# Windowed attention in a decoder layer: the weighted sums of values computed per half of a query block, with a difference over 64 keys in quarters of the TensorE array

## The chip, the core and the metric

The kernel runs on one core of one Trainium2 chip. Five engines work side by side, each with its own instruction queue: TensorE (PE in the profile; PEld are its weight loads), VectorE (DVE), ScalarE (ACT), GpSimd (POOL) and SyncE (SP, which here only issues DMAs). The metric is the time of one execution in microseconds on the device; less is better.

## What is computed

One decoder layer over 2048 tokens of width 1024. A joint input projection feeds a sliding-window attention (8 query heads, 2 key/value heads, width 64, blocks of 128 queries) and a convolution group; both are joined by an output projection, and a gated feed-forward network follows, each with root-mean-square norms around it. The part that matters here is the attention, in the reference:

```
kb, vb = band(kp), band(vp)            # previous block and own block: 256 keys
s = einsum("bnqhgd,bnkhd->bnhgqk", qb, kb) * scale
dist = qi + BLOCK - kj                 # qi: 0..127, kj: 0..255
in_band = (dist >= 0) & (dist < WINDOW)   # WINDOW = BLOCK = 128
s = where(valid, s + bias, -inf)
...
p = (p / denom)
o = einsum("bnhgqk,bnkhd->bnqhgd", p, vb)
```

With a window of 128 and blocks of 128, query q of a block sees exactly 128 keys: keys 0 to q of its own block, and keys q+1 to 127 of the previous block. So for each key place k from 0 to 127 there is one weight: it belongs to the own block's key k where k <= q, and to the previous block's key k where k > q.

## The kernel before

The layer runs in stages over four groups of 512 tokens. Stage A is the projections (PSUM banks `mm`, four of them), stage B the attention, C the convolution's taps on VectorE and its tail, J a product of two weight matrices, W the output projection and first norms, H and F the start of the feed-forward network, G its end. Stages A, W, J and F are long runs of matmuls of 128x128 weights by 512 columns. Stage B and the others are written as generators and woven into these runs in lanes; at the end a scheduler with a timeline of its own (`schedule_with_timeline_sim=True`, L1635) decides each engine's order from priorities and from when tiles come free. Each engine then runs its queue strictly in that order.

Stage B (`stage_b`, L465) has four blocks of 128 queries for each of the four groups, sixteen in all. For each block:

- `front(b)`, L472: two groups of score matmuls (output `tr@B`, inputs `kz` and `ql@A`, 64 rows of the array for each key/value head `g`, twelve matmuls a group, in one PSUM bank for each `g`), then VectorE keeps for each key place the score of the block it belongs to (L501), adds the bias and takes maxima (L504), and ScalarE takes exponentials (L524).
- `back(b)`, L531: VectorE forms `vd`, the previous block's values less the own block's (128x128, L538 through the helper at L85); it divides the weights by their sum; for each of the two heads `g`, TensorE turns four 128x128 pieces (L546), ScalarE copies the bank to `pg[:, 1]` (L547), which holds all weights with keys on partitions and 4 x 128 queries as columns, and GpSimd makes `pg[:, 0]` from it, the same with zeros where k <= q (L549).
- Then the weighted sum (L567 through `mat`, L108): in one bank, own values times all weights plus `vd` times the masked weights. `g` takes one half of the array's columns, since the values of a head are 64 wide. This is four matmuls of 128 rows, 64 columns of weights and 512 columns of data; they are plain float32, and each stands in the trace as two records. ScalarE copies the bank to `at` (L576) and issues its DMA to `mixT` (L578).
- The very first block of all has no previous block; it has only the two matmuls with the own values.

The banks called `tr` (L75) are three; the transposes of a block, its weighted sum and the score groups take them in turn. A score group needs two.

Of the kernel before, what the change touches and what calls it, by code (L numbers as in the profile page):

```python
# [17 lines left out]
AF = mybir.ActivationFunctionType  # L18
ALU = mybir.AluOpType
# [6 lines left out]
P = 128  # L26
# [2 lines left out]
KC = D // P  # L29
NF = DFF // P  # L30
TAPS = 31
HALO = TAPS - 1
EPS = 1e-6
NEG = -1e30
# [3 lines left out]
def layer_kernel(ctx, tc, x, xT, cols, rows, sinks, relb, onehot, w_in, w_four, w_pw, w_out, w_gate, w_up, w_down, out):  # L38
    nc = tc.nc
# [35 lines left out]
    tr = lambda: bank("tr", 3)  # L75
# [3 lines left out]
    act = nc.scalar.activation  # L79
# [27 lines left out]
    def mat(*args, **kw):  # L107
        r = nc.tensor.matmul(*args, **kw)  # L108
        if not inlane[0]:
            lead_pe[0] = r  # L110
        return r
# [353 lines left out]
    def stage_b(t):  # L465
        L = f"B{t}"
        q = qs[t]

        def freed(r):
            done_.append(r)  # L470

        def front(b):  # L472
            lab[0] = L
            first = t == 0 and b == 0
            tok = slice(b * P, (b + 1) * P)
            win = slice(b * P, b * P + 256)
            mx = sm(8)
            pr = f4("p", (P, 8, P))
            for ip in range(2):
                os = [tr().rearrange("p (j k) -> p j k", j=2) for _ in range(2)]  # L480
                lead = []
                pq = tc.cur_priority
                for j in range(2):
                    i = 2 * ip + j
                    for n, (a, k) in enumerate(((0, 0), (0, 1), (1, 0))):
                        for g in (1, 0):
                            sl = slice(64 * g, 64 * g + 64)
                            if lead:
                                tc.cur_priority = pq - 10000
                            r = mat(os[g][:, j], q[i][sl, a, tok], kz[sl, k, win], start=n == 0, stop=n == 2)  # L490
                            if lead:
                                after_first(lead[-1], r)
                            else:
                                for x_ in done_[-3:][:2]:
                                    after_first(x_, r, mybir.DependencyClass.Sync)
                            if len(lead) < 2:
                                lead.append(r)
                tc.cur_priority = pq + 1
                for g in range(2):
                    prev = neg.unsqueeze(2).to_broadcast([P, 2, P]) if first else os[g][:, :, 0:P]  # L500
                    nc.vector.copy_predicated(os[g][:, :, P:], upper.unsqueeze(1).to_broadcast([P, 2, P]), prev)  # L501
                    for j in range(2):
                        h = 4 * g + 2 * ip + j
                        read = nc.vector.tensor_tensor_reduce(  # L504
                            out=pr[:, h],
                            in0=os[g][:, j, P:],
                            in1=bias[0][:, h],
                            op0=ALU.add,
                            op1=ALU.max,
                            scale=1.0,  # L510
                            scalar=NEG,
                            accum_out=mx[:, h : h + 1],
                        )
# [12 lines left out]
            rd = sm(8)  # L526
            nc.vector.reciprocal(rd, den)
            live[b] = pr, rd
            yield YC

        def back(b):  # L531
            pr, rd = live.pop(b)
            first = t == 0 and b == 0
            pt = []
            if not first:
                lab[0] = L
                vd = t_("vd", (P, P))
                vtt(vd, vtok[:, b], vtok[:, b + 1], ALU.subtract)  # L538
            for g in range(2):
                lab[0] = L  # L540
                hs = slice(4 * g, 4 * g + 4)
                vtt(pr[:, hs], pr[:, hs], rd[:, hs].unsqueeze(2).to_broadcast([P, 4, P]), ALU.mult)
                pg = f4("p", (P, 2, T))
                o = tr()
                for i in range(4):
                    nc.tensor.transpose(o[:, i * P : (i + 1) * P], pr[:, 4 * g + i], ident)  # L546
                freed(act(pg[:, 1], o, AF.Copy))  # L547
                if not first:
                    nc.gpsimd.affine_select(  # L549
                        out=pg[:, 0].rearrange("p (i q) -> p i q", q=P),  # L550
                        in_=pg[:, 1].rearrange("p (i q) -> p i q", q=P),
                        compare_op=ALU.is_gt,
                        fill=0.0,
                        base=0,
                        pattern=[[0, 4], [-1, P]],
                        channel_multiplier=1,
                    )
                pt.append(pg)
                yield 0.9
            yield YP  # L560
            lab[0] = L
            o = tr()
            lead = None
            for kb in (1,) if first else (0, 1):
                for g in (1, 0):
                    sl = slice(64 * g, 64 * g + 64)
                    r = mat(o[sl], vtok[:, b + 1, sl] if kb else vd[:, sl], pt[g][:, kb], start=first or kb == 0, stop=kb == 1)  # L567
                    if lead is None:
                        lead = r
                        pq = tc.cur_priority  # L570
                        tc.cur_priority = pq - 10000
                    else:
                        after_first(lead, r)
            tc.cur_priority = pq
            at = f2("at")
            freed(act(at, o, AF.Copy))  # L576
            c0 = t * T + b * P
            nc.scalar.dma_start(  # L578
                mixT[0:4, :, c0 : c0 + P].rearrange("c p t -> p c t"), at.rearrange("p (c t) -> p c t", c=4)
            )  # L580
            yield 1.8

        live = {}

        def scores():
            for b in range(4):
                yield from front(b)
                if 0 < b < 3:
# [1051 lines left out]
```

## Time and profile before

| | |
|---|---|
| time, median of 3 runs | 1907.33 us (1906.63 to 1907.36) |
| profiled execution: span from first to last instruction | 1907.9 us; its own time is not listed beside it |
| granted TensorE clock | 0.999 |
| instructions in the span | 26569 |
| ACT busy | 970.6 us (51%) |
| POOL busy | 179.2 us (9%) |
| weighted sums, records on PE | 64 with `vtok`, 60 with `vd` |
| first and last weighted sum start | 128.2 us and 552.9 us |
| score groups, records on PE | 384, from 77.2 us to 521.3 us |

Busy shares of an engine say how much of the span it had work in hand. TensorE's matmuls are pipelined, so their recorded lengths overlap: a record of a 512-column matmul lasts about 390 ns while the next one starts about 227 ns after it. What a matmul costs is therefore read from where the next one starts, not from its length.

### The profile page before, as it was taken

What the parts mean: (1) busy time and instruction counts of PE and PEld (TensorE: products, weight loads), DVE (VectorE), ACT (ScalarE), POOL (GpSimd) and SP (SyncE); (2) the same over time, 40 slices, a digit from 0 to 9 for tenths busy, and PEclk for the clock granted to TensorE, in tenths of its full rate; (3) what the DMA queues carried; (4) which work ended last, traced back from release to release, by engine and by line L of the source; (5) the groups of instructions that cost most, each with busy time, mean ns of one, the idle gap of its engine ahead of it and who ended that gap; (6) DMA issues with size and microseconds to landing.
All of it is one profiled execution on the core that took longest, in us unless ns stands there. A gap on an engine that the chain in (4) does not pass through costs nothing.

```text
span 1907.9 us, 26569 instructions
## 1 busy us (share of the span) xinstructions
PE 1889.1 (99%) x8714; PEld 1530.1 (80%) x8714; DVE 1490.7 (78%) x2721; ACT 970.6 (51%) x1912; POOL 179.2 (9%) x196
## 2 busy tenths in 40 slices
PE   9999999999999999999999999999999999999998
PEld 8777777777777888888888878788888888888886
DVE  6999999987966999999996765887567674455558
ACT  5356445566667433433445574685443433345452
POOL 2010001110000000000000000010033233211002
PEclk9999999999999999999999999999999999999999
DMA  9887746679688677877776596798554443375663
GB/s 353 300 281 238 248 160 207 230 228 318 218 274 276 232 234 232 293 261 243 244 268 195 196 326 212 259 333 307 166 176 156 160 138 127 116 258 187 206 220 133
DMA packets 226491, 439.29 MB, mean 230 GB/s; under 512 B 22536, under 2 KB 48560, under 8 KB 226352
## 3 DMA queue, kind: packets, MB, share of 16 engines
q1 hardware_dynamic: 207344, 411.37, 64.8%
q10 hardware_dynamic: 17088, 19.93, 2.9%
q0 software_dynamic: 1920, 6.29, 0.9%
q8 instruction: 68, 1.11, 0.2%
q14 instruction: 71, 0.58, 0.1%
HBM read 318.48 MB, written 119.02 MB: 229 GB/s over the span
## 4 chain that ended last, share of the span: by engine, by line
PE 78%; DVE 9%; DMA 8%; ACT 3%; issue 2%; SPq 0%; ACTq 0%; DVEq 0%; POOL 0%; POOLq 0%
PE mm@F L108 34%; PE mm@G L108 16%; PE mm@A L108 14%; PE tr@W L108 5%; PE mm@W L108 3%; PE tr@B L108 2%; PE ct@J L108 1%; DVE w@F L85 1%; DVE mid@W L85 1%; DMA hl@A<-x 1%; DVE sm@G L85 1%; DVE y2@C L85 1%; DMA chl@H<-hT 1%; DVE hl@G L85 1%; DMA chl@F<-w_gate 1%
## 5 line engine op out<-in xcount | busy, mean ns | idle before, releaser
L108 PE MATMUL mm@F<-hl@H,w@F 128*128 128x512 f32 x1056 | 255.8, 391 | 1.8 <-ACT mm@F L1058 1.6
L108 PEld LDWEIGHTS mm@F<-hl@H,w@F 128*128 128x128 f32 x1056 | 197.7, 188 | 44.8 <-ACT mm@F L1058 2.8
L108 PE MATMUL mm@G<-hl@G,hl@G 128*128 128x512 f32 x924 | 226.1, 393 | 2.3 <-ACT hl@G L904 1.5
L904 ACT ACTIVATE w@F<-chl@F 128x512 fp32r<-128x512 f32 x220 | 136.5, 626 | 170.2 <-PE mm@F L108 158.7
L108 PEld LDWEIGHTS mm@G<-hl@G,hl@G 128*128 128x128 f32 x924 | 171.5, 188 | 39.7 <-ACT hl@G L904 2.2
L108 PE MATMUL mm@G<-w@G,hl@G 128*128 128x512 f32 x876 | 199.8, 389 | 0.6 <-DVE w@G L85 0.6
L108 PEld LDWEIGHTS mm@G<-w@G,hl@G 128*128 128x128 f32 x876 | 164.3, 188 | 35.2 <-DVE w@G L85 1.0
L108 PE MATMUL mm@A<-hl@A,w@A 128*128 128x512 f32 x792 | 192.2, 394 | 0.0
L108 PEld LDWEIGHTS mm@A<-hl@A,w@A 128*128 128x128 f32 x792 | 146.8, 188 | 32.5 <-issue 1.7
L85 DVE TENSOR_TENSOR w@F<-chl@F,w@F 128x512 fp32r<-128x512 f32 x198 | 148.1, 753 | 25.5 <-ACT w@F L904 25.0
L85 DVE SCALAR_TENSOR_TENSOR y2@C<-g2@C,colt,y2@C 128x1024 f32<-128x1024 f32 x120 | 154.0, 1283 | 0.2
L108 PE MATMUL mm@F<-mid@H,w@F 128*128 128x512 f32 x528 | 130.6, 390 | 1.0 <-DVE w@F L85 0.9
L108 PE MATMUL mm@F<-ql@H,w@F 128*128 128x512 f32 x528 | 129.7, 390 | 0.2
L108 PE MATMUL mm@F<-p@H,w@F 128*128 128x512 f32 x528 | 129.1, 389 | 0.0
L108 PE MATMUL mm@F<-x@H,w@F 128*128 128x512 f32 x528 | 127.8, 390 | 0.0
L108 PEld LDWEIGHTS mm@F<-mid@H,w@F 128*128 128x128 f32 x528 | 98.8, 188 | 22.2 <-DVE w@F L85 1.3
L108 PEld LDWEIGHTS mm@F<-ql@H,w@F 128*128 128x128 f32 x528 | 98.7, 188 | 21.3 <-DVE w@F L85 0.6
L108 PEld LDWEIGHTS mm@F<-x@H,w@F 128*128 128x128 f32 x528 | 98.7, 188 | 21.3 <-issue 0.8
L108 PEld LDWEIGHTS mm@F<-p@H,w@F 128*128 128x128 f32 x528 | 99.1, 188 | 20.6
L133 ACT ACTIVATE w@A<-raw@A 128x512 fp32r<-128x512 f32 x100 | 60.9, 625 | 80.2 <-PE mm@A L108 46.3
L85 DVE TENSOR_TENSOR w@G<-raw@G,w@G 128x512 fp32r<-128x512 f32 x72 | 50.2, 698 | 64.2 <-ACT w@G L904 63.4
L108 PE MATMUL mm@W<-w@W,hl@W 128*128 128x512 f32 x384 | 97.1, 399 | 0.8 <-DVE x@W L85 0.4
(322 smaller groups left out, 3363.9 us busy)
## 6 DMA issues: line engine op xcount, KB each, us to landing
mids<-fa@F SPq DMA_DIRECT2D x154, 256.0 KB, 3.3
raw@A<-w_in SPq DMA_DIRECT2D x50, 512.0 KB, 4.9
w@A<-lo_in SPq DMA_DIRECT2D x84, 256.0 KB, 4.0
fa@G<-mids SPq DMA_DIRECT2D x74, 256.0 KB, 4.7
fc@G<-mids SPq DMA_DIRECT2D x72, 256.0 KB, 3.5
w@W<-lo_out SPq DMA_DIRECT2D x48, 256.0 KB, 4.8
chl@F<-w_gate SPq DMA_DIRECT2D x22, 512.0 KB, 4.4
raw@F<-w_gate SPq DMA_DIRECT2D x22, 512.0 KB, 4.2
```

Of the source, the lines that this page charges most:

```text
L85: r = op(*args, **kw)
L108: r = nc.tensor.matmul(*args, **kw)
L133: act(w[:, 0], raw, AF.Copy)
L904: act(w[:, 0], x, AF.Copy)
```

## The change

For the first 64 queries of a block (half n = 0), keys 64 to 127 always belong to the previous block; for the last 64 queries (n = 1), keys 0 to 63 always belong to the own block. So the base of half 0 is now the previous block's values and the base of half 1 the own block's, and the difference is needed only over 64 keys: keys 0 to 63 for half 0, keys 64 to 127 for half 1, with opposite signs. The sums of the two halves go to two banks of 256 columns each. A difference matmul then has 64 rows, 64 columns of weights and 256 columns of data, a quarter of the array; a base matmul has 128 rows, 64 columns and 256 columns of data. `vd` is made by two VectorE instructions on 64 partitions each, the masked weights by two GpSimd instructions of half the columns each, and ScalarE copies two banks of 256 columns instead of one of 512.

```diff
@@ stage_b
+        def quarter(pg, kb, n):
+            return pg[:, kb].rearrange("p (i q) -> p i q", q=P)[:, :, H * n : H * n + H]
...
                 vd = t_("vd", (P, P))
-                vtt(vd, vtok[:, b], vtok[:, b + 1], ALU.subtract)
+                vtt(vd[0:H], vtok[0:H, b + 1], vtok[0:H, b], ALU.subtract)
+                vtt(vd[H:P], vtok[H:P, b], vtok[H:P, b + 1], ALU.subtract)
...
                 if not first:
-                    nc.gpsimd.affine_select(
-                        out=pg[:, 0].rearrange("p (i q) -> p i q", q=P),
-                        in_=pg[:, 1].rearrange("p (i q) -> p i q", q=P),
-                        compare_op=ALU.is_gt,
...
+                    for n, cmp in enumerate((ALU.is_ge, ALU.is_gt)):
+                        nc.gpsimd.affine_select(
+                            out=quarter(pg, 0, n),
+                            in_=quarter(pg, 1, n),
+                            compare_op=cmp,
+                            fill=0.0,
+                            base=-H * n if n else 0,
+                            pattern=[[0, 4], [-1 if n else 1, H]],
+                            channel_multiplier=1 if n else -1,
+                        )
...
-            o = tr()
+            os = [tr()[:, 0 : 4 * H] for _ in range(2)]
             lead = None
             for kb in (1,) if first else (0, 1):
-                for g in (1, 0):
-                    sl = slice(64 * g, 64 * g + 64)
-                    r = mat(o[sl], vtok[:, b + 1, sl] if kb else vd[:, sl], pt[g][:, kb], start=first or kb == 0, stop=kb == 1)
...
+                for n in range(2):
+                    for g in (1, 0):
+                        sl = slice(H * g, H * g + H)
+                        rows_ = slice(0, P) if kb else slice(H * n, H * n + H)
+                        v = vtok[:, b + (n or first), sl] if kb else vd[rows_, sl]
+                        r = mat(os[n][sl], v, quarter(pt[g], kb, n)[rows_], start=first or kb == 0, stop=kb == 1)
...
             at = f2("at")
-            freed(act(at, o, AF.Copy))
+            for n in range(2):
+                freed(act(at.rearrange("p (i q) -> p i q", q=P)[:, :, H * n : H * n + H],
+                          os[n].rearrange("p (i q) -> p i q", q=H), AF.Copy))
```

`H` is 64. The scheduler places the eight matmuls of a block in three ways. The lists below are TensorE's queue; in them `tr@B_224` and so on are banks, `p@B` the weights of one head, `mm@A`, `mm@F` outputs of stages A and F, and a row's size is that of its output. The helper `mat` stands at L108 before and at L109 after the change.

First, the last block of the first 512 tokens. Before, its sum and the start of the next score group:

```order
L108 MATMUL mm@A_344_2184<-hl@A_284_1812,w@A_343_2181 128x512 x2
L108 MATMUL tr@B_281_1795<-p@B_272_1737,vd@B_269_1725 64x512
L108 MATMUL tr@B_281_1795<-p@B_270_1728,vd@B_269_1725 64x512
L108 MATMUL tr@B_281_1795<-p@B_272_1737,vtok 64x512
L108 MATMUL tr@B_281_1795<-p@B_270_1728,vtok 64x512
L108 MATMUL tr@B_313_1996<-kz,ql@A_268_1722 128x256
```

The same place with the change:

```order
L109 MATMUL mm@A_348_2215<-hl@A_295_1892,w@A_347_2212 128x512 x3
L109 MATMUL tr@B_284_1820<-p@B_275_1761,vd@B_272_1747 64x256
L109 MATMUL tr@B_284_1820<-p@B_273_1751,vd@B_272_1747 64x256
L109 MATMUL tr@B_285_1821<-p@B_275_1761,vd@B_272_1747 64x256
L109 MATMUL tr@B_285_1821<-p@B_273_1751,vd@B_272_1747 64x256
L109 MATMUL tr@B_284_1820<-p@B_275_1761,vtok 64x256
L109 MATMUL tr@B_284_1820<-p@B_273_1751,vtok 64x256
L109 MATMUL tr@B_285_1821<-p@B_275_1761,vtok 64x256
L109 MATMUL tr@B_285_1821<-p@B_273_1751,vtok 64x256
L109 MATMUL mm@A_363_2295<-hl@A_265_1703,w@A_361_2289 128x512 x3
```

All four difference matmuls stand together, then the four base matmuls; nine of the fifteen blocks that have a difference are like this. The score group that came straight behind the sum now comes later, with 19 projection matmuls ahead of it. Over the whole queue, eight sums were followed straight by a score group before, and one is now.

Second, the second block of all, with the change (before, its four matmuls stood together, with a score group straight behind):

```order
L109 MATMUL tr@B_225_1448<-p@B_223_1439,vd@B_215_1383 64x256
L109 MATMUL tr@B_225_1448<-p@B_216_1387,vd@B_215_1383 64x256
L109 MATMUL tr@B_225_1448<-p@B_223_1439,vtok 64x256
L109 MATMUL tr@B_225_1448<-p@B_216_1387,vtok 64x256
L109 MATMUL mm@A_282_1792<-mid@A_104_714,w@A_280_1786 128x512
...
L109 MATMUL mm@A_282_1792<-chl@A_127_871,w@A_281_1789 128x512
L109 MATMUL tr@B_226_1449<-p@B_223_1439,vd@B_215_1383 64x256
L109 MATMUL tr@B_226_1449<-p@B_216_1387,vd@B_215_1383 64x256
L109 MATMUL tr@B_226_1449<-p@B_223_1439,vtok 64x256
L109 MATMUL tr@B_226_1449<-p@B_216_1387,vtok 64x256
L109 MATMUL tr@B_237_1510<-kz,ql@A_99_694 128x256
```

The two halves stand apart, with 17 projection matmuls between them. Three blocks are split like this (the others with 3 and with 8 matmuls between the halves).

Third, the last block of all. Before:

```order
L108 MATMUL tr@B_977_5660<-p@B_972_5632,vd@B_969_5620 64x512
L108 MATMUL tr@B_977_5660<-p@B_970_5623,vd@B_969_5620 64x512
L108 MATMUL tr@B_977_5660<-p@B_972_5632,vtok 64x512
L108 MATMUL tr@B_977_5660<-p@B_970_5623,vtok 64x512
L108 MATMUL mm@F_1017_5908<-x@H_863_5137,w@F_1007_5844 128x512 x3
```

With the change:

```order
L109 MATMUL tr@B_992_5793<-p@B_987_5764,vd@B_984_5750 64x256
L109 MATMUL tr@B_992_5793<-p@B_985_5754,vd@B_984_5750 64x256
L109 MATMUL tr@B_992_5793<-p@B_987_5764,vtok 64x256
L109 MATMUL tr@B_992_5793<-p@B_985_5754,vtok 64x256
L109 MATMUL tr@B_993_5794<-p@B_987_5764,vd@B_984_5750 64x256
L109 MATMUL tr@B_993_5794<-p@B_985_5754,vd@B_984_5750 64x256
L109 MATMUL tr@B_993_5794<-p@B_987_5764,vtok 64x256
L109 MATMUL tr@B_993_5794<-p@B_985_5754,vtok 64x256
```

The halves follow each other without other work between them, but each half's base stands ahead of the other half's difference. The last three blocks are like this (in the first of them one base matmul of half 0 stands ahead of the difference of half 1, the other behind it).

More of the change, by code (lines that the diff above doesn't have):

```diff
@@ L31 @@
 TAPS = 31
+H = P // 2
 HALO = TAPS - 1
@@ L548, in back @@
                 if not first:
-                    nc.gpsimd.affine_select(
-                        out=pg[:, 0].rearrange("p (i q) -> p i q", q=P),
-                        in_=pg[:, 1].rearrange("p (i q) -> p i q", q=P),
-                        compare_op=ALU.is_gt,
[L553 to L557, printed above, removed]
+                    for n, cmp in enumerate((ALU.is_ge, ALU.is_gt)):
[8 more added lines that the diff above has]
+                        )
                 pt.append(pg)
@@ L561, in back @@
             lab[0] = L
-            o = tr()
+            os = [tr()[:, 0 : 4 * H] for _ in range(2)]
             lead = None
             for kb in (1,) if first else (0, 1):
-                for g in (1, 0):
-                    sl = slice(64 * g, 64 * g + 64)
-                    r = mat(o[sl], vtok[:, b + 1, sl] if kb else vd[:, sl], pt[g][:, kb], start=first or kb == 0, stop=kb == 1)
[L568 to L573, printed above, removed]
+                for n in range(2):
[4 more added lines that the diff above has]
+                        r = mat(os[n][sl], v, quarter(pt[g], kb, n)[rows_], start=first or kb == 0, stop=kb == 1)
+                        if lead is None:
+                            lead = r
+                            pq = tc.cur_priority
+                            tc.cur_priority = pq - 10000
+                        else:
+                            after_first(lead, r)
             tc.cur_priority = pq
             at = f2("at")
-            freed(act(at, o, AF.Copy))
+            for n in range(2):
+                freed(act(at.rearrange("p (i q) -> p i q", q=P)[:, :, H * n : H * n + H],
+                          os[n].rearrange("p (i q) -> p i q", q=H), AF.Copy))
             c0 = t * T + b * P
```

## The prediction

> **What bounds the kernel now.** I read the busy times first, then what TensorE (PE) waited for, then the timeline of one weighted sum. The page's first part:
>
> ```profile
> PE 1889.1 (99%) x8714; PEld 1530.1 (80%) x8714; DVE 1490.7 (78%) x2721; ACT 970.6 (51%) x1912; POOL 179.2 (9%) x196
> ```
>
> PE's recorded lengths overlap, so 99% alone proves little. The view of waits, for PE over the whole span, has fourteen rows; the first and the last two are
>
> ```profile
> PE ct@X L108 <- POOL ident masks.py:199: 1.6, 1, 1.6
> ...
> PE mm@F L108 <- ACT gb@F L1159: 0.2, 1, 0.2
> PE tr@B L546 <- DVE sm@B L504: 0.2, 1, 0.2
> ```
>
> They fall from 1.6 to 0.2 us and together make about 10 us of 1907.9. PE has work nearly everywhere, so what counts is how long its own queue takes: a microsecond that the change adds to that queue or takes from it is a microsecond of the result. The sums are few:
>
> ```profile
> L108 PE MATMUL tr@B<-p@B,vtok 128*64 128x512 f32 x64 | 16.5, 594 | 0.0
> L108 PE MATMUL tr@B<-p@B,vd@B 128*64 128x512 f32 x60 | 16.2, 618 | 0.0
> ```
>
> 33 us of PE in all, of which the difference (`vd`) is half. Halving that half could not gain more than 8 us, 0.4%.
>
> What one sum costs is read from starts. This is PE's timeline, and that of its weight loads, at the second block:
>
> ```profile
> 152.00 1.29 PE L108 MATMUL mm@A<-chl@A,w@A 128*128 128x512 f32 x5
> 153.22 1.08 PE L108 MATMUL tr@B<-p@B,vd@B 128*64 128x512 f32 x4
> 154.13 1.03 PE L108 MATMUL tr@B<-p@B,vtok 128*64 128x512 f32 x4
> 155.09 0.97 PE L108 MATMUL tr@B<-kz,ql@A 64*128 64x256 f32 x12
> 155.99 1.19 PE L108 MATMUL mm@A<-chl@A,w@A 128*128 128x512 f32 x4
> ```
> ```profile
> 153.22 0.20 PEld L108 LDWEIGHTS tr@B<-p@B,vd@B 128*64 128x64 f32 x4 [0.35 <-issue]
> 153.70 0.14 PEld L108 LDWEIGHTS tr@B<-p@B,vtok 128*64 128x64 f32 x2 [0.29 <-issue]
> 154.13 0.14 PEld L108 LDWEIGHTS tr@B<-p@B,vtok 128*64 128x64 f32 x2 [0.28 <-issue]
> ```
>
> Two matmuls (one for each head, in the two column halves) are four records, and they run in **rounds** of two at a time: the loads for the base come at 153.70 and 154.13, one round or 0.43 us apart. From the first `vd` record to the first `vtok` record is 0.91 = two rounds and 0.05; from there to the score group 0.96 = two rounds and 0.10. Ahead of the sum, five projection records of about 0.39 us start within 1.29 - 0.39 = 0.90, so every 0.225; the last starts at 152.90, and the sum 0.32 behind it, 0.095 more than the rule. So **entering** this shape costs 0.095 + 0.05 = 0.145 us and **leaving** it 0.10. Behind the score group four projection records take 1.19 - 0.39 = 0.80 for three steps instead of 0.675: the first weights of a new shape, 128 columns wide, cost another 0.125, against 0.05 for 64 columns. A change back to 128x128 is then about 0.22, one to the score shape (weights of 128 columns too) about 0.2. Between rounds of one shape nothing of this is paid.
>
> The Trainium skill has this as a rule: in "TensorEngine Tiling (Array Packing)", section "Tiling Modes", a change of tiling mode, not merely of the tile, drains the TensorE. The 0.095 and 0.10 at these borders agree. It names no price; with a drain alone, without the weights' 0.05, the inner changes below would be 24 x 0.095 = 2.3 us and the sum +1.4.
>
> **The change, term by term.**
>
> 1. *Streaming.* A round of 256 columns should be half of 0.43, 0.215 us. In nine blocks the four quarter matmuls stand together, and I take them to run all four at once: two rounds of 0.215 instead of two of 0.43, -0.43 each, **-3.9**. In the six others (three split, three with the halves in a row) only two difference matmuls are neighbours: four rounds of 0.215, 0.86 as before. In one of these a base matmul of half 0 is cut off from its partner: ten rounds of 0.215 = 2.15 against 4 x 0.43 = 1.72, **+0.4**. The base of all sixteen blocks goes from two rounds of 0.43 to four of 0.215: nothing. No row shows a plain float32 round of 256 columns. A projection step, one pass of 512 columns, takes 0.225, and half a plain float32 round of 512 columns 0.215; if each short round had that 0.01 as a fixed part, 108 rounds would add 1.1; less than half of 0.43 is excluded, since the columns still have to pass. I take 0, since the rounds of 0.43 are the nearest row. That four quarters run at once is not in the trace either: two column halves do (above), and two row halves do, as twelve score records in 0.97 us show, 0.28 us being the last one's own length:
>
> ```profile
> L108 PE MATMUL tr@B<-kz,ql@A x384: 271/277/385, 77.2 to 521.3; 64*128 64x256 f32 x192
> ```
>
>    Its ends are two rounds (-3.9) and four (0).
>
> 2. *Changes of shape inside a sum.* The difference (64 rows) and the base (128 rows) are now different shapes. The order has 24 such borders: one in each of nine blocks, two in each split block, three in each of the last three. From below 0, if a change of rows alone is free; from above 0.22, the dearest border seen. I take 0.145, as for entering this shape with the same 64 columns of weights: **+3.5** (0 to 5.3).
>
> 3. *Split blocks.* A second entry and a second return to 128x128 in three blocks: 3 x (0.145 + 0.22) = **+1.1**.
>
> 4. *Score groups that move away.* Eight groups started straight behind a sum, sharing its border. Seven now stand behind projection matmuls: the sum returns to 128x128 (0.22 for 0.2), and the group has a border of its own, 7 x 0.2, with the rounding **+1.5**.
>
> Together -3.9 + 0.4 + 3.5 + 1.1 + 1.5 = **+2.6 us** on PE.
>
> The other engines:
>
> ```profile
> L85 DVE TENSOR_TENSOR vd@B<-vtok x15: 273/283/292, 95.0 to 514.4; 128x128 f32<-128x128 f32 x15
> L576 ACT ACTIVATE at@B<-tr@B 128x512 f32<-128x512 f32 x16 | 9.4, 590 | 12.0 <-PE tr@B L108 12.0
> L549 POOL TENSOR_SCALAR_AFFINE_SELECT p@B<-p@B x30: 633/838/1802, 142.6 to 552.2; 128x512 f32<-128x512 f32 x30
> 148.05 0.87 POOL L549 TENSOR_SCALAR_AFFINE_SELECT p@B<-p@B 128x512 f32<-128x512 f32 x1 [4.47 <-ACT p@B L547]
> ```
>
> DVE makes `vd` in two instructions of the same 128 columns on 64 partitions: between 0 and 0.28 more for each block, 4.2 us in all. It is formed early (the first at 95.0, for the sum at 153.2), and DVE's queue is filled up by convolution taps that nothing waits for at once, so I count 0. That cover is thin in two stretches:
>
> ```profile
> 144.00:192.00 48.00, 48.00 (x233) 36.72 (x232) 47.89 (x107) 29.81 (x77) 3.31 (x3) 1.00 0.74 243
> 288.00:336.00 48.00, 48.00 (x252) 36.99 (x251) 47.75 (x105) 26.76 (x61) 6.62 (x10) 1.00 0.68 214
> ```
>
> The third figure of time is DVE's, full to 0.3 us; four sums lie there, so 4 x 0.28 = 1.1 if the cover fails. ScalarE's copy becomes two of 256 columns, each between half and all of 0.59: 0 to +9 us on an engine that is half idle; 0. GpSimd's select becomes two of 256 columns, again between half and all of 0.84; in this block it ended at 148.9, 4.3 us ahead of the sum, so even doubled it is hidden.
>
> **Rivals.**
>
> *The four quarters go two at a time.* Term 1 loses its -3.9: +6.5, **1913.8**, slower. For it: no row shows four at once, and each matmul brings two records that must follow each other. Against it: in the old sum those records pair up across column halves. It decides at the nine blocks: the four rounds take 0.86 rather than 0.43. Chance 15%.
>
> *Starts strictly in program order, one matmul behind the other.* If only neighbouring records of different matmuls overlapped, four matmuls of two records would take five rounds: nine blocks x 3 x 0.215 = +5.8 on the forecast, **1915.7**. By the same count the old sum would take five rounds of 0.43, 2.15 us, where 1.87 (153.22 to 155.09) stands in the trace, so 4%. The Trainium skill's "TensorE: Matmul & The Clock Gate", Part 3, says that matmuls start and end in program order; by that rule this is what would come if the two records of a matmul stand side by side, and the trace speaks against that reading.
>
> *Borders inside a sum are free*, since the column halves stay as they are. Term 2 is gone: -0.9, **1906.4**. For it: no such border is in the trace. Against it: every border that is (three shapes, both ways) costs at least 0.095. Chance 13%.
>
> *Score groups wait for a bank.* The sums hold two of the three `tr` banks, and a score group needs two; it must wait for ScalarE's copy of half 0. At the second block that copy came late, behind exponentials:
>
> ```profile
> 157.84 0.58 ACT L576 ACTIVATE at@B<-tr@B 128x512 f32<-128x512 f32 x1
> ```
>
> 2.75 us after the sum was done at 155.09. In the new order 12 to 19 matmuls at 0.225, 2.7 to 4.3 us, lie between, which mostly covers it. If ScalarE ran 1 us later than that at half of the eight places, +4: **1914.0**. It decides where the copy ends more than 2.7 us behind the sum. Chance 12%.
>
> **How the numbers follow.** The profiled execution's span of 1907.9 goes to 1910.5. The median of the runs shown is 1907.33, 0.6 lower, so I add the 2.6 there: **1909.9 us**, +0.14%, with 56% for this case and 1908 to 1912 as its own width (rounds up to +1.1, thin cover on DVE up to +1.1, waits that come and go as the order of the first 560 us is dealt anew, about 1 either way). A measurement of this kernel can tell about 0.2%, 3.8 us, from no change: 1903.5 to 1911.1. Within it lie seven tenths of the forecast (39%), nearly all of the free borders (12%) and a little of the rest (2%): 53%. Slower: the rest of the forecast and nearly all of the other three rivals, 43%. Faster needs free borders and more besides, 4%. The range from **1906.0** to **1915.0** takes in the two bounds of term 2 and of the four quarters.
>
> **What would show it.** In the changed profile a block of the first kind should run from the start of its first `vd` record to the next other matmul in about 0.265 + 0.31 + 0.265 + 2 x 0.215 + 0.31 = 1.58 us (before 1.87); the `vd` rounds should hold four starts within some 0.02 us. A split block should take about 1.16 us for each half, the last block about 2.3. The mean length of a record will fall and tell nothing. I am wrong if `vd` starts come in pairs 0.215 apart, if `vtok` starts 0.215 rather than 0.31 behind the last `vd` round, or if PE's waits in the first 560 us grow by more than 2 us.

## The result, and the profile after

The changed kernel takes **1926.53 us** (median of 4 runs, 1923.52 to 1928.29); the kernel before, beside it, 1907.18 us (1906.63 to 1907.36). The ratio is 1.0100, with a 95% interval of 1.0088 to 1.0112: slower by 1.0%. The profiled run took 1926.28 us with a span of 1924.6; 16.7 us more span than before is what has to be found. That is less than the 19.3 us between the medians: in every run that lists both, the span is 1.6 to 1.9 us below the time, so the execution profiled before took some 1909.6 us by this estimate, 2.4 over the median. In the changed kernel the helpers stand at L109 and L86, the transposes at L551, the copy to `pg` at L552, the selects at L555, the copy to `at` at L586.

The page's busy times:

```profile
PE 1897.7 (99%) x8838; PEld 1538.6 (80%) x8838; DVE 1495.2 (78%) x2736; ACT 976.4 (51%) x1930; POOL 193.6 (10%) x226
```

PE is still at 99%, and no engine's work has grown by 16 us. The first thing to check is the sums themselves. PE's timeline at a block whose quarters stand together, and at a half of one whose halves are split (start, length, what it is):

```profile
183.01 0.66 PE L109 MATMUL tr@B<-p@B,vd@B 64*64 64x256 f32 x8
183.61 1.08 PE L109 MATMUL tr@B<-p@B,vtok 128*64 128x256 f32 x8
184.62 0.73 PE L109 MATMUL mm@A<-hl@A,w@A 128*128 128x512 f32 x2
...
505.25 0.65 PE L109 MATMUL tr@B<-p@B,vd@B 64*64 64x256 f32 x4
505.83 0.65 PE L109 MATMUL tr@B<-p@B,vtok 128*64 128x256 f32 x4
506.41 0.66 PE L933 MATMUL ct@H<-ident,fa@H 128*128 128x128 f32 x4
```

From the first `vd` record to the next other matmul the first block takes 184.62 - 183.01 = 1.61 us; 1.58 was forecast, 1.87 stood there before. The single starts in the trace are 0, 0.006, 0.013, 0.020, then 0.266 to 0.286, then 0.592 for the first base matmul: four quarters at once, in rounds 0.267 apart, and 0.325 from the second round over the border to the base. A split half takes 506.41 - 505.25 = 1.16, as forecast, and the last block takes 2.32 (2.3). So these sums do what the prediction says (those that did not are counted below), and most of the loss is elsewhere. The view of PE's waits has fifteen rows; the first eight are

```profile
PE mm@A L109 <- DVE ql@A L86: 3.0, 1, 3.0
PE tr@B L109 <- POOL p@B L555: 2.5, 4, 1.1
PE mm@G L109 <- ACT hl@G L915: 2.0, 2, 1.3
PE ct@C L625 <- DMA fc@C<-y_scr: 1.9, 1, 1.9
PE ct@X L109 <- POOL ident masks.py:199: 1.6, 1, 1.6
PE ct@C L625 <- ACT yt@C L626: 1.4, 2, 1.0
PE mm@W L109 <- ACT mid@W L781: 0.9, 1, 0.9
PE mm@W L109 <- ACT hl@W L806: 0.9, 1, 0.9
```

Before, the longest was 1.6 us and neither `ql@A` nor `POOL p@B` was in the list. The largest wait stands at 291.9 us. PE's timeline there, after (its last row is cut off at 301 us by the window of the view) and then before:

```profile
288.40 0.39 PE L109 MATMUL mm@A<-hl@A,w@A 128*128 128x512 f32 x1
288.72 0.97 PE L109 MATMUL tr@B<-kz,ql@A 64*128 64x256 f32 x12
289.62 0.66 PE L625 MATMUL ct@C<-ident,fc@C 128*128 128x128 f32 x4
291.23 0.66 PE L625 MATMUL ct@C<-ident,fc@C 128*128 128x128 f32 x4 [0.95 <-ACT yt@C L626]
294.94 6.38 PE L109 MATMUL mm@A<-hl@A,w@A 128*128 128x512 f32 x15 [3.05 <-DVE ql@A L86]
```
```profile
283.76 5.15 PE L108 MATMUL mm@A<-hl@A,w@A 128*128 128x512 f32 x22
288.75 0.49 PE L614 MATMUL ct@C<-ident,fc@C 128*128 128x128 f32 x3
289.17 0.98 PE L108 MATMUL tr@B<-kz,ql@A 64*128 64x256 f32 x12
290.08 0.66 PE L546 MATMUL tr@B<-ident,p@B 128*128 128x128 f32 x4
290.58 0.27 PE L614 MATMUL ct@C<-ident,fc@C 128*128 128x128 f32 x1
290.61 5.27 PE L108 MATMUL mm@A<-hl@A,w@A 128*128 128x512 f32 x22
```

Before, 22 projection matmuls cover the time ahead of the score group and 22 more the time behind it. After, one stands ahead, then turned tiles, and the next projection matmul needs a bank that VectorE empties late: its queue brings `ql@A` at 294.19, behind the taps (`y2@C`) and the score group's own selection (L505):

```profile
286.90 0.55 DVE L86 TENSOR_SCALAR y2@C<-glu@C,colt 128x512 f32<-128x512 f32 x1 [1.87 <-DMA glu@C<-glu_scr]
...
288.15 0.58 DVE L86 TENSOR_TENSOR vd@B<-vtok 64x128 f32<-64x128 f32 x2
288.76 2.33 DVE L86 SCALAR_TENSOR_TENSOR y2@C<-glu@C,colt,y2@C 128x512 f32<-128x512 f32 x3
291.01 1.29 DVE L86 TENSOR_TENSOR mid@A<-x@A,mid@A 128x512 fp32r<-128x512 f32 x2
...
292.87 0.76 DVE L505 COPY_PREDICATED tr@B<-upper,tr@B 128x256 f32<-128x256 int8 x2
...
294.19 0.69 DVE L86 SCALAR_TENSOR_TENSOR ql@A<-mm@A,ql@A 128x512 fp32r<-128x512 f32 x1
```

VectorE is busy from 286.90 on, so PE waits for a full queue and not for an idle engine; 1.87 us of that lateness is its wait for a DMA just ahead. The wait has a tail. The view by windows (span, then busy time of PE, PEld, DVE, ACT, POOL, then the granted clock) shows the stretch behind it, and the 48 us around it:

```profile
288.00:294.00 6.00, 2.93 (x24) 1.93 (x22) 5.88 (x12) 3.17 (x6) 0.00 (x0) 0.99 0.67 182
294.00:300.60 6.60, 5.66 (x13) 4.46 (x14) 5.24 (x15) 0.14 (x1) 0.00 (x0) 0.50 0.21 79
```
```profile
288.00:336.00 48.00, 44.00 (x225) 33.73 (x225) 42.92 (x97) 24.78 (x58) 7.07 (x12) 0.93 0.58 174
```

At half the clock (all but the last of them start within it) 15 projection matmuls take 6.38 us, where 22 took 5.27. In these 48 us PE gets through 225 records, before 252.

For all kernels below I added up PE's queue in one way: each step from one record's start to the next, less the undisturbed step of its kind (0.227 us for 512 columns, 0.109 for a turned tile, 0.059 for a score record). That rule gives 1831.0 us to every kernel in the table; what goes beyond it is sorted. "Sums" is all that their records take when nothing holds them, with the border into each sum and out of it, "borders" up to 0.11 us at any other change of shape, "waits" single steps more than 0.15 too long ("inside sums" also holds those just ahead of one), and "half clock" the excess in stretches of clock 0.5. Some 10 us of smaller excess, alike in all to about 2 us, are left out.

| kernel | time, us | sums | borders | waits, first 620 us | waits, later | waits inside sums | half clock |
|---|---|---|---|---|---|---|---|
| before | 1907.2 | 30.5 | 6.4 | 11.1 | 7.8 | 0 | 0 |
| after | 1926.5 | 33.2 | 7.0 | 18.5 | 6.5 | 3.2 | 4.1 |

Sums and borders: +3.3 us. Waits and half clock: 7.4 - 1.3 + 3.2 + 4.1 = **+13.4**. Four fifths of the loss are not in the sums' own time.

### The profile page after: what moved, and what is told of

Its sections match the earlier page's. It is cut to its first block, busy times and chain, and to the rows that moved or that the text cites. A ratio compares the mean times of both kernels' runs of the same rounds, so it can differ in the third digit from the quotient of the medians.

```text
span 1924.6 us, 26893 instructions
## 1 busy us (share of the span) xinstructions
PE 1897.7 (99%) x8838; PEld 1538.6 (80%) x8838; DVE 1495.2 (78%) x2736; ACT 976.4 (51%) x1930; POOL 193.6 (10%) x226
## 4 chain that ended last, share of the span: by engine, by line
PE 72%; DVE 16%; DMA 8%; issue 3%; ACT 1%; SPq 0%; POOL 0%; DVEq 0%; ACTq 0%; POOLq 0%
PE mm@F L109 33%; PE mm@G L109 18%; PE mm@A L109 9%; PE tr@W L109 5%; DVE y2@C L86 3%; PE mm@W L109 3%; DVE fc@C L86 2%; PE tr@B L109 2%; DMA wx@G<-w_down 1%; DMA mixT<-fc@C 1%; DMA glu@C<-glu_scr 1%; DVE w@F L86 1%; DVE chl@F L86 1%; DMA fa@G<-mids 1%; DVE sm@G L86 1%
## 5 line engine op out<-in xcount | busy, mean ns | idle before, releaser
L109 PE MATMUL mm@F<-hl@H,w@F 128*128 128x512 f32 x1056 | 256.4, 392 | 0.2 <-ACT gb@F L1170 0.2
L109 PEld LDWEIGHTS mm@F<-hl@H,w@F 128*128 128x128 f32 x1056 | 198.6, 189 | 42.6 <-issue 0.8
L109 PE MATMUL mm@G<-hl@G,hl@G 128*128 128x512 f32 x924 | 225.8, 393 | 2.6 <-ACT hl@G L915 2.0
L109 PEld LDWEIGHTS mm@G<-hl@G,hl@G 128*128 128x128 f32 x924 | 171.6, 188 | 39.6 <-ACT hl@G L915 2.6
L109 PE MATMUL mm@G<-w@G,hl@G 128*128 128x512 f32 x876 | 199.8, 389 | 0.6 <-DVE w@G L86 0.6
L109 PE MATMUL mm@A<-hl@A,w@A 128*128 128x512 f32 x792 | 195.1, 398 | 3.0 <-DVE ql@A L86 3.0
L109 PEld LDWEIGHTS mm@G<-w@G,hl@G 128*128 128x128 f32 x876 | 164.3, 188 | 35.2 <-DVE w@G L86 1.0
L109 PEld LDWEIGHTS mm@A<-hl@A,w@A 128*128 128x128 f32 x792 | 149.3, 191 | 36.5 <-DVE ql@A L86 3.3
L86 DVE TENSOR_TENSOR w@F<-chl@F,w@F 128x512 fp32r<-128x512 f32 x198 | 147.2, 749 | 28.3 <-ACT w@F L915 27.9
L86 DVE SCALAR_TENSOR_TENSOR y2@C<-g2@C,colt,y2@C 128x1024 f32<-128x1024 f32 x120 | 154.6, 1289 | 0.2
L109 PE MATMUL mm@F<-mid@H,w@F 128*128 128x512 f32 x528 | 130.5, 390 | 0.7 <-ACT fa@F L1180 0.7
L109 PE MATMUL mm@F<-ql@H,w@F 128*128 128x512 f32 x528 | 129.8, 391 | 0.3
L109 PE MATMUL mm@F<-p@H,w@F 128*128 128x512 f32 x528 | 129.1, 389 | 0.0
L109 PE MATMUL mm@F<-x@H,w@F 128*128 128x512 f32 x528 | 128.0, 391 | 0.0
L109 PEld LDWEIGHTS mm@F<-mid@H,w@F 128*128 128x128 f32 x528 | 98.8, 188 | 22.0 <-ACT fa@F L1180 1.1
L109 PEld LDWEIGHTS mm@F<-ql@H,w@F 128*128 128x128 f32 x528 | 98.7, 188 | 21.4 <-DVE w@F L86 0.6
L109 PEld LDWEIGHTS mm@F<-p@H,w@F 128*128 128x128 f32 x528 | 99.1, 188 | 20.6
L109 PEld LDWEIGHTS mm@F<-x@H,w@F 128*128 128x128 f32 x528 | 98.6, 188 | 21.0 <-DVE sm@W L86 0.4
L86 DVE TENSOR_TENSOR w@G<-raw@G,w@G 128x512 fp32r<-128x512 f32 x72 | 51.1, 710 | 64.6 <-ACT w@G L915 63.8
L109 PE MATMUL mm@W<-w@W,hl@W 128*128 128x512 f32 x384 | 98.6, 399 | 1.8 <-ACT mid@W L781 0.9
```

The costliest lines, as they stand in the source:

```text
L86: r = op(*args, **kw)
```

## The experiments

Kernels of one group ran on one chip, and each is compared with the kernel before beside it: 1906.11 us in the first group (experiments 1 and 2), 1909.3 in the second (3, without its last kernel), 1907.76 over 15 runs in the third (that kernel, 4 and 6), 1909.29 in the fourth (5). All but the last are single executions, so 3 or 4 us between two of them are not read.

**1. The order dealt anew, with no work changed.** The lanes of stage B yield with numbers that say how much other work may pass; one such number was changed in the kernel before.

```diff
-    YP = 1.5
+    YP = 2.5
```


> The kernel before, same instructions and same sizes, with the sums emitted 1 us later in their lane (YP 2.5 for 1.5), so that the scheduler deals the first 600 us anew. Reshuffle theory (any new order costs, because the old one happens to meet the late transfers well): 1912 to 1922 us, with new waits of PE in the first 600 us, at other places. Own-cost theory (the selects, the banks and the borders of the change make PE wait): 1906 to 1909 us.

1918.79 us: +12.7, with the same arithmetic. Three rows of its waits say why:

```profile
PE tr@B L108 <- POOL p@B L549: 5.7, 2, 3.5
PE mm@W L108 <- DVE vtok L448: 2.4, 1, 2.4
PE tr@B L546 <- ACT p@B L547: 2.2, 1, 2.2
```

In this order the old kernel, too, waits for GpSimd's select (838 ns at the median in the order as given), and its clock, too, falls to 0.5: three times for 3.4 us, from 331.3, 389.3 and 546.3 us, each time behind a step that was 2.4 to 2.6 us too long. So the 1907 us hold for one order among several.

**2. One part at a time.** Two selects of 256 columns in the kernel before:

```diff
-                    nc.gpsimd.affine_select(out=pg[:, 0]..., compare_op=ALU.is_gt, base=0, pattern=[[0, 4], [-1, P]], channel_multiplier=1)
+                    for n in range(2):
+                        nc.gpsimd.affine_select(out=quarter(pg, 0, n), in_=quarter(pg, 1, n), compare_op=ALU.is_gt, fill=0.0,
+                            base=-H * n if n else 0, pattern=[[0, 4], [-1, H]], channel_multiplier=1)
```


> The kernel before with the masked weights made by two selects of 256 columns instead of one of 512; same values. Own-cost theory with the selects as the cause: a pair takes 1.47 us instead of 0.88 (the mean of 60 in the changed kernel is 0.73), PE waits for POOL by 2 us and more in all, 1910 to 1914 us. Reshuffle theory: anything from 1907 to 1918 us, and PE's waits for POOL stay under 1 us.

Two banks, with 256-column sums of 128 rows and two copies, but one select and the old base and difference:

```diff
-            o = tr()
+            os = [tr()[:, 0 : 4 * H] for _ in range(2)]
...
+                        rows_ = slice(0, P)
+                        v = vtok[:, b + 1, sl] if kb else vd[rows_, sl]
```


> The kernel before with the sums in two banks of 256 columns each and two copies by ScalarE, but difference and base over all 128 rows (no quarters, one select, one vd). PE's own work: sums as before, score groups that move away +1.5 us, split blocks +0.35 each. Own-cost theory with the banks as the cause: 1912 to 1920 us. If only the selects count: 1908.5 to 1910.5 us. Reshuffle theory: 1909 to 1920 us.

The changed kernel with the halves in the other order:

```diff
-                for n in range(2):
+                for n in (1, 0):
                     for g in (1, 0):
```


> The changed kernel with the halves in the other order (half 1 first, whose bank and whose masked weights come last), which leaves 14 of 15 blocks together and one split: 16 borders between difference and base for 24. PE's own work falls by about 14 x 0.43 - 9 x 0.43 + 8 x 0.145 + 0.7 = 4 us against the changed kernel. If the borders and order of the sums were the loss: 1915 us or less, with PE's waits for POOL gone. Reshuffle theory: 1922 less or more 6 us, by where the new order waits.

They took 1902.38, 1911.51 and 1928.83 us: -3.7, +5.4 and +22.7 against the kernel before. The first lies below every range that was expected of it and the last above, the second in the range for a mere new order. The last one is the sharpest. It happens to put the four quarters together in 14 of 15 blocks, each 1.61 us long, and its sums fall to 27.4 us, 3.1 less than before: the gain that the change can give is there in full. But PE's waits in the first 620 us are 26.9 us, and the time is worse than the changed kernel's. So the time of the quarters themselves is not what costs.

**3. Twins: the same step in both kernels.** If the loss were only luck of the order, it should vanish on average over other orders.

```diff
-    YC = 3
+    YC = 3.5
```


> The kernel before with another neutral step of its lanes (YC 3.5 for 3, the pause between scores and sum), same instructions. Reshuffle theory: again another time with no work changed, 1903 to 1920 us, and PE's own work (steps without waits) as before within 1.5 us. Own-cost theory: 1905 to 1908 us.

> The changed kernel with the same neutral step (YC 3.5). Reshuffle theory: 1908 to 1926 us, as far from the other kernels as they are from each other. Own-cost theory: 1924 to 1930 us, like the changed kernel, and 17 to 21 us above its twin without the change (YC 3.5).

> The changed kernel with the sums emitted 1 us later (YP 2.5). Its twin without the change took 1918.8 us. Own-cost theory: 19 us above the twin, 1936 to 1940 us. Reshuffle theory: 1910 to 1930 us; on PE's own work alone (+2.6 us) it would stand at 1921 us.


```diff
-                yield 0.9
+                yield 1.1
             yield YP
```


> The kernel before with the smallest of the neutral steps (a lane pause of 1.1 for 0.9 behind each turned head; some 250 places of PE's order differ). Reshuffle theory: 1903 to 1915 us. Own-cost theory: 1905 to 1908 us.

> The changed kernel with the smallest neutral step (1.1 for 0.9); its twin without the change took 1909.8 us. Two lasting stalls of two banks: both there. Time 1918 to 1930 us; on PE's own work alone it would be 1912 to 1913.

| step | old kernel, us | its difference | changed kernel, us | its difference | change less old |
|---|---|---|---|---|---|
| as given | 1907.2 | 0 | 1926.5 | +19.3 | +19.3 |
| YP 2.5 | 1918.8 | +12.7 | 1920.3 | +11.0 | -1.7 |
| YC 3.5 | 1911.5 | +2.2 | 1922.4 | +13.1 | +10.9 |
| 1.1 for 0.9 | 1909.8 | +0.5 | 1927.5 | +19.7 | +19.2 |

Each difference is taken to the unchanged kernel before of the same group. In three orders of four the changed kernel is clearly slower than its twin, in one they are level; the mean of the last column is +12. The changed kernel stands between 11 and 20 us above the 1907 in every order, the old one between 0 and 13. Luck is large, but most likely not all; four orders are few to say it by.

**4. The change put together step by step.** Two banks and two selects; then also `vd` in two halves, which is all of the change except the quarters (every difference matmul still has 128 rows):

```diff
                 vd = t_("vd", (P, P))
-                vtt(vd, vtok[:, b], vtok[:, b + 1], ALU.subtract)
+                vtt(vd[0:H], vtok[0:H, b], vtok[0:H, b + 1], ALU.subtract)
+                vtt(vd[H:P], vtok[H:P, b], vtok[H:P, b + 1], ALU.subtract)
```


> Two banks and two selects, but difference and base over all 128 rows and one vd. Theory that the second bank makes two lasting stalls (behind the turned conv tail near 290 us, waiting for VectorE's ql, and near 510 us, turned stage-H tiles waiting for ScalarE): both are there, 1.5 us or more each. Theory that banks and selects together make the rest of the loss: PE waits for POOL at sums, 1918 to 1925 us. Theory that only the quarter shape and reshuffling make the rest: 1908 to 1914 us, like the two banks alone (1911.5).

> All of the change except the quarter shape: two banks, two selects, two halves of vd, two copies, but 128 rows in every matmul. PE's queue differs from the changed kernel's only in the shape of the differences and in where the scheduler puts things. If the parts around the sums make the loss: 1920 to 1928 us, PE's waits ahead of 600 us some 18 to 25 us as in the four quarter kernels (11 to 14 in the one-bank ones). If the quarters themselves make it: 1909 to 1914 us.

1915.83 and 1922.52 us, +8.1 and +14.8: the first falls between the ranges expected of it, the second into the range for the parts around the sums. In the same account:

| kernel | time, us | sums | borders | waits, first 620 us | waits, later | waits inside sums | half clock |
|---|---|---|---|---|---|---|---|
| two selects | 1902.4 | 30.5 | 6.5 | 7.5 | 4.1 | 1.0 | 0 |
| two banks | 1911.5 | 31.1 | 7.0 | 13.1 | 5.0 | 0 | 1.4 |
| two banks, two selects | 1915.8 | 31.2 | 7.0 | 16.4 | 6.4 | 0.1 | 0 |
| all but the quarters | 1922.5 | 31.9 | 7.1 | 19.5 | 5.0 | 2.7 | 2.8 |
| changed, halves reversed | 1928.8 | 27.4 | 7.2 | 26.9 | 5.7 | 1.5 | 4.4 |
| YP 2.5, before | 1918.8 | 30.8 | 6.5 | 13.4 | 4.9 | 7.3 | 3.2 |
| YP 2.5, changed | 1920.3 | 31.8 | 7.0 | 19.7 | 4.4 | 0.6 | 2.7 |

Without the quarters' shape the loss is already 15 us of the 19. The wait for `ql@A` is longer in it than in the changed kernel (PE's timeline):

```profile
291.36 0.66 PE L625 MATMUL ct@C<-ident,fc@C 128*128 128x128 f32 x4
293.19 0.66 PE L625 MATMUL ct@C<-ident,fc@C 128*128 128x128 f32 x4 [1.18 <-ACT yt@C L626]
298.20 2.07 PE L109 MATMUL mm@A<-hl@A,w@A 128*128 128x512 f32 x4 [4.36 <-DVE ql@A L86]
```

Two places were the same in kernel after kernel: turned tiles of `ct@C` and then `mm@A` waiting for `ql@A` (at 288 to 299 us, 0.85 to 4.4 us long), and `ct@H` and `mm@W` waiting for ScalarE (504 to 520 us, 1.1 to 1.8 us together). All eight kernels up to here that sum into two `tr` banks have both; none of the five with one bank (before, its three twins, two selects) has either. Two selects alone make nothing slower; that they add to the loss of two banks (+8.1 for +5.4) is less than single executions can tell.

**5. The bank.** That made the second held bank the suspect, and three kernels were to test it: the kernel before with one `tr` bank fewer, and the changed kernel with the second half's sums in a bank of the projections, in two orders.

```diff
-    tr = lambda: bank("tr", 3)
+    tr = lambda: bank("tr", 2)
```


> The kernel before with two tr banks instead of three, no work changed. Theory (the second held tr bank displaces the score groups and so makes TensorE wait): with a bank less all the time the same two stalls appear as in every kernel that sums into two banks, turned tiles of ct@C and then mm@A waiting for VectorE's ql@A at 280 to 300 us, and ct@H and mm@W waiting for ScalarE at 504 to 520 us; time at least 1912. Rival (any re-dealing of the order moves the time by some us, the number of tr banks has no part in it): neither stall, time somewhere between 1904 and 1919 like the other re-dealt kernels.


```diff
-            os = [tr()[:, 0 : 4 * H] for _ in range(2)]
+            os = [bank_of()[:, 0 : 4 * H] for bank_of in (tr, mm)]
```


> The changed kernel with the second half's sums in one of the four mm banks of the projections, so that only one tr bank is held by a sum. Theory (tr banks): neither of the two stalls at 280 to 300 and 504 to 520 us; TensorE's waits before 620 us fall from 18.5 to 11 to 14, and the time to 1912 to 1918, unless the projections wait for their bank instead. Rival (the late selects and the order at large, not the bank): both stalls or others of their size stay, time 1920 to 1930.

> The same with the step before the sums 2.5 instead of 1.5, which gives the same arithmetic in another order. Theory: below the 1920.3 of the changed kernel with this step, by 3 to 8 us. Rival: within 3 us of 1920.3 or above.

A bank fewer: 1974.46 us, 65 more with no work changed. That is not all stage B's loss. Stage H turns its tiles in `tr` banks too (`tr@H`, up to 1397.7 us), and the three longest rows of PE's waits are of that later time (the longest of each at 668, 1318 and 1328 us):

```profile
PE mm@F L108 <- ACT w@F L904: 11.8, 2, 10.6
PE tr@H L922 <- DMA at@H<-hn_scr: 6.6, 2, 5.1
PE mm@F L108 <- ACT mid@H L945: 6.3, 1, 6.3
```

By the rule of the account, PE's steps lose 27.9 us more than before up to 620 us (the last sum starts at 610.8), and 37.0 more behind it. In both parts some of it is the clock, which stands at 0.50 for 64.8 us ahead of the kernel's end, 37.6 of them behind 620 us. What the run says of stage B is thus about 28 us. The second place shows up (PE waits 0.78, 1.23 and 0.55 us at 519 to 523 us), the first does not: at 302 us `ct@C` waits for a DMA, and the wait for `ql@A` is at 175 us, behind a score group that itself came late:

```profile
169.69 1.34 PE L108 MATMUL tr@B<-p@B,vd@B 128*64 128x512 f32 x4 [4.14 <-POOL p@B L549]
170.82 1.93 PE L108 MATMUL tr@B<-p@B,vtok 128*64 128x512 f32 x4
172.67 0.58 PE L108 MATMUL tr@B<-kz,ql@A 64*128 64x256 f32 x1
173.43 1.65 PE L108 MATMUL tr@B<-kz,ql@A 64*128 64x256 f32 x11 [0.18 <-ACT at@B L576]
177.05 1.22 PE L108 MATMUL mm@A<-mid@A,w@A 128*128 128x512 f32 x2 [1.97 <-DVE ql@A L85]
```

The bank taken from the projections was no remedy. The first of the two kernels gives an output that is off by 3%, for a reason that was not found, so its time is not read; the second took 1966.18 us, +56.9, where the changed kernel with this step has +11.0 and 3 to 8 less than that was expected. Of the two places it has only the second, although its sums hold a single `tr` bank. They now stand right behind the transposes, and PE meets GpSimd's selects, the first row of its waits:

```profile
PE tr@B L109 <- POOL p@B L555: 15.3, 6, 3.8
```

So a missing `tr` bank costs much, in stage B and behind it, and a missing `mm` bank too; that the second held bank is the one cause of the 13 us is not shown. A kernel with four `tr` banks and nothing else given up was not tried, since all eight banks are in use.

**6. The part that paid, timed.** The two selects alone, executed 11 times.

> The kernel before with two selects, timed: its one look gave 1902.4 beside 1906.1. If an order can be lucky as well as unlucky, it stays 2 to 5 us below the kernel before (ratio 0.9975 to 0.999), with GpSimd busier by 16 us in all and no other work changed; if that look was chance, the ratio is 1.000.

1903.79 us (11 runs, 1902.17 to 1905.94) against 1907.76 (15 runs), a ratio of 0.9981 with an interval of 0.9972 to 0.9990: faster than both kernels by a little. It adds GpSimd time and takes none from PE; what falls are PE's waits (11.1 to 7.1 us in the first 620 us and 7.8 to 6.0 later, by the account). Behind the wait of 1.6 us at the program's start, the next in its list are

```profile
PE mm@G L109 <- ACT hl@G L909: 1.4, 1, 1.4
PE tr@B L109 <- POOL p@B L554: 0.9, 1, 0.9
```

By experiment 1 a gain of this size can come from the order alone, and whether the shorter selects or their order give it was not separated.

## Why the prediction was wrong

The forecast was 1909.9 us, +2.6, within 1906 to 1915; it came to 1926.5. Of its three signs of being wrong, the first two did not come and the third did: PE's waits, which were not to grow by more than 2 us in the first 560 us, went from 11.1 to 18.5 us in the first 620 us, without those inside sums. By its own steps:

- **Streaming (-3.9 + 0.4).** Right as a mechanism: four quarters run at once, at 0.267 + 0.325 + 0.267 + 0.216 + 0.216 + 0.316 = 1.607 us for a block, 0.03 over the forecast. Of the nine blocks five ran so. In two the second half's quarters start 0.18 us late, and in two a wait for GpSimd pulls the halves apart (1.22 us at 282 us, 0.56 at 469), so they lose the overlap.
- **Borders (+3.5), split blocks (+1.1), score groups (+1.5).** Near. Difference to base costs 0.11 over the round as it stands between 0.267 and 0.592 (0.325 - 0.215), and the first round of the base another 0.05 (0.267 for 0.215): 0.16, of 0.145 forecast; a split half 1.161; the last block 2.324. The Trainium skill says in "TensorEngine Tiling (Array Packing)", section "Tiling Modes", that a change of tiling mode drains the TensorE. The 0.11 agrees with it. All terms on PE's own work, with the nine blocks as they ran, give +3.3 in the account above, for +2.6. That they come so close is in part luck: as far as the account separates them, the sums with their own borders took 2.7 more (forecast -3.9 + 0.4 + 3.5, and 0.7 of the split blocks' term, together +0.7), the borders elsewhere 0.6 more (the rest of the forecast, +1.9). What the score groups cost by themselves was not measured.
- **Quarters two at a time**, **strict order**, **free borders:** the first two are excluded by the starts, four within 0.020 us, the third by the 0.16.
- **Score groups wait for a bank.** As put, no: no row of the changed kernel has a score group waiting for ScalarE's copy `at@B`. It happens once each in three others (1.1 us with YC 3.5, 1.3 with YP 2.5, 0.5 with the halves reversed). In the changed kernel the groups stand further from the sums; that this is what it pays for in other places is argued, not shown.
- **The step that failed** is "waits that come and go as the order of the first 560 us is dealt anew, about 1 either way". Measured, +13.4 us of waits and half clock. The prediction had two facts that spoke against it: VectorE full to 0.3 us in two of the windows, and a list of waits that was only 10 us long although its feeders had so little slack. It read the second as PE's own queue being all that counts, and priced the order at about 1 us, less than the longest wait that was there (1.6), and not at the waits that could come. One re-dealing of the old kernel moves it by 12.7 us.
- **GpSimd, "even doubled it is hidden".** Wrong in two ways. Half the columns are not half the time, and the lead differs by block: 4.3 us in the block looked at, none at 282 us. The view of one line:

```profile
L555 POOL TENSOR_SCALAR_AFFINE_SELECT p@B<-p@B x60: 404/740/1877, 143.9 to 576.3; 128x256 f32<-128x256 f32 x60
```
```profile
280.50 3.37 POOL L555 TENSOR_SCALAR_AFFINE_SELECT p@B<-p@B 128x256 f32<-128x256 f32 x2 [9.87 <-ACT p@B L552]
282.43 0.65 PE L109 MATMUL tr@B<-p@B,vd@B 64*64 64x256 f32 x4 [0.36 <-POOL p@B L555]
283.92 0.65 PE L109 MATMUL tr@B<-p@B,vd@B 64*64 64x256 f32 x4 [0.84 <-POOL p@B L555]
```

  Median 740 ns against 838 for twice the columns. There the two selects took 3.37 us, and PE waited for each of them. It cost 2.5 us in all by the list of waits.
- **VectorE's `vd`.** The halves take 288 ns each (median), against 283 for the whole in the prediction's row: the upper end, 4.2 us more. They lie in a queue that PE waits for at 291.9 us, and adding the halves to two banks and two selects went with +6.7 us.
- **ScalarE's copies**, 383 ns each instead of 590: no wait of PE for them stands in the changed kernel's list, as forecast. Whether the 0.18 us more for each block delays ScalarE's other work, for which PE does wait (`yt@C`, `hl@W`), was not separated.

What stays open is how the 13 us divide. Two banks, late selects and `vd` halves each went with a loss, in the order of adding (+5, +3, +7, and +5 with the quarters), but the first three are single executions and each step deals the order anew, which alone moves the old kernel by up to 12.7. Shown is that the quarters' own time doesn't cause it and that 15 us of the 19 stand without their shape, that the changed kernel loses in all four of its orders more than 10 us, where the old one does so in one, and that the kernel has no `tr` bank to spare. Why the second bank should lead to the two recurring waits is argued from the order (score groups moved away from the sum, the projection matmuls between them used up, VectorE's queue with `ql@A` behind them), and the test of it was not clean.

## What to carry to other kernels

Where one engine is busy 99% of the time because a scheduler has fitted everything else under it, price a change by what it does to the lead of the work that feeds that engine (banks held, shorter producers, fuller queues), and take the spread of a few neutral re-orderings of the old kernel as the width of the forecast, before counting single matmuls. Then judge the change over several orders in both kernels, since the same two kernels here differed by anything from -1.7 to +19.3 us. An instruction of half the columns was not half the price here, so splitting work among small instructions on the feeding engines must be paid from their slack.

## What the hardware showed beside that

- **The clock halves at some waits.** During the wait of 3.05 us that starts at 291.9 us the granted clock fell to 0.50, from 293.9 us on and for 6.8 us, and again for 3.4 us from 567.0, 2 us behind a wait of 1.1 us for GpSimd. Behind one of 1.9 us for a DMA, at 388 us, it stayed at 1.00, and so it did in the old kernel with YP 2.5 behind a step at 367 us that was 3.6 us too long. Before, it fell only at the kernel's very end. This is a third kind of cost, 4.1 us in all, that no row of waits lists. The row for the second place:

```profile
567.00:570.40 3.40, 3.40 (x10) 2.17 (x9) 2.74 (x4) 1.67 (x2) 0.00 (x0) 0.50 0.39 131
```

- **GpSimd's select of 256 columns** ran from 0.40 to 1.88 us, the longest at 280.5 us while VectorE was busy 4.47 of 4.50 us; two of them cost 1.5 us on average (60 with a mean of 733 ns), where one of 512 columns cost 0.88.
